# Moving three small tiles so that all large tiles of a hybrid decoder layer start at one remainder of 512 bytes

## The chip, the cores and the metric

The kernel runs on one core of a Trainium2 chip. The metric is the device time of one execution in microseconds; lower is better. A time shown is the median of several executions.

## The reference

One layer of a hybrid decoder on 512 tokens of width 1024, in float32. A normed input goes through one wide projection; a block-sparse attention branch and a gated linear recurrence branch follow; they are merged by sigmoid gates, projected, added to the input, and a gated embedding is added.

```python
xn = rmsnorm(h, norm_gain)
aq, ak, av, ag, bq, bf, bi, bg, gate_a, gate_b = split(xn @ w_in)    # 8 parts of 512 columns, 2 of 1024
ya = moba_attention(rmsnorm(aq) , rmsnorm(ak), av, rel_bias)          # 8 heads of 64
ya = (ya * silu(ag)) @ w_up_a
yb = hgrn2_chunkwise(silu(bq), (1 - lb) * sigmoid(-bf), bi, log_f)    # 4 heads of 128
yb = (rmsnorm(yb, hgrn_out_gain) * silu(bg)) @ w_up_b
h = h + (sigmoid(gate_a) * ya + sigmoid(gate_b) * yb) @ w_out
h = h + (p @ w_ple) * sigmoid(h @ w_ple_gate)
```

## The kernel before

Activations lie transposed: 128 features on the partitions, 512 tokens along the free axis, one tile of 2048 bytes a partition for each 128 features. Every large product is made of three TensorE matmuls in a reduced float32 format, high part by high part, high by low, low by high. So each operand exists as a high and a low tile: `wh`, `wl` for weights, `gh`, `gl` for the input times its gain, `xh`, `xl` for the normed input, `ybh`, `ybl` and `yah`, `yal` for the two branches, `mh`, `ml` for the merged value, `hh`, `hl` for the sum after the output projection, `ph`, `pl` and `pwh`, `pwl` for the embedding and its weights. ScalarE makes the high part by a copy, VectorE the low part by a subtraction (`split`, `scale_split`, `w_split`).

A projection of 128 output features is `mm3`, 8 blocks of 128 input features times 3 matmuls, 24 in all, each with 128 stationary columns and 512 moving ones. There are two orders. `proj_tr` (bf, bq, bg, ag, ga, gb), `up` (ub, ua) and the last two stages (h, g) hold a 128-column slice of the weights stationary and move the activations. `proj_tok` (bi, av, aq, ak) holds 128 tokens of the activations stationary and moves 512 weight columns. The last block of g is done in two halves of 256 columns.

Weights come by DMA from the SyncE queue into two `w` buffers, and are split two tiles ahead of their use into three buffers each for `wh` and `wl`. TensorE's order is written out by hand (`ORDER`, and generators that `tick` starts at due times); the other engines' order is set by a scheduler with priorities. Between the projections TensorE works on small matmuls of the attention (`s`, scores; `pt`, transposes of the softmax weights p; `o`, values) and of the recurrence (`lpb`, `lpa`, `hktp`, `hds`, `hop`).

`column_norms` sums a 128x512 tile over the partitions: a transpose of 32x32 blocks, a reduction to 128x16, three additions of 32-row groups, an inverse square root, and the way back. It is called five times, once for the input (`x_norm`) and once for each head of the recurrence (`hgrn_out`). Its three tiles of 128x16 (`sums`, `y`, `t_`; 64 bytes a partition) come from tag `n16` of the pool `sb`, with 3 buffers.

The pool `cst` lies ahead of the pool `sb` in SBUF; within a pool the tiles lie one after the other, in `sb` by tag in the order in which tags are first used, so each tag's place follows from the sizes of those ahead of it.

Of the kernel before, what the change touches and what calls it, by code (L numbers as in the profile page):

```python
# [11 lines left out]
F32 = mybir.dt.float32  # L12
# [45 lines left out]
def hybrid_layer_kernel(  # L58
# [18 lines left out]
    cst = ctx.enter_context(tc.tile_pool(name="cst", bufs=1))  # L77
# [4 lines left out]


    BUFS = {"w": 2, "wh": 3, "wl": 3, "A": 16, "R": 4, "X": 16, "YB": 8, "H": 10, "T": 3, "Q": 4, "QM": 2, "QX": 2, "KT": 2, "P": 4, "PT": 2,
            "PT0": 2, "PT2": 2, "SG": 4, "YS": 1, "VV": 8, "s32": 1, "st": 1, "ps": 8, "n16": 3}

    def unit(tag, name, dt=F32, shape=(128, 512)):
        return sb.tile(list(shape), dt, tag=tag, bufs=BUFS[tag], name=name)

    def bank(tag, name):  # L90
        return psum.tile([128, 512], F32, tag=tag, bufs={"mm": 4, "g": 2, "a": 2}[tag], name=name)
# [169 lines left out]
    def rsqrt(y, t, ms):  # L261

        A.activation(t, ms, AF.Ln, bias=epsc[0:t.shape[0], 0:1])
        A.activation(y, t, AF.Exp, scale=-0.5)
        V.scalar_tensor_tensor(t, ms, EPS, y, op0=OP.add, op1=OP.mult)
        V.tensor_tensor(t, t, y, op=OP.mult)
        V.tensor_scalar(t, t, -0.5, 1.5, op0=OP.mult, op1=OP.add)
        V.tensor_tensor(y, y, t, op=OP.mult)
# [15 lines left out]

    gh, gl, xh, xl = [], [], [], []
    rt = cst.tile([128, NT], F32, name="rt")

    def x_gain(k0, k1):
        for k in range(k0, k1):
            h_ = unit("A", f"gh{k}", R)  # L290
            l_ = unit("A", f"gl{k}", R)
            scale_split(h_, l_, xr[k], gain[:, k:k + 1])
            gh.append(h_)
            gl.append(l_)
# [26 lines left out]
    def column_norms(src, n, name, tag):  # L321


        u = unit(tag, name + "u")
        sums = unit("n16", name + "s", shape=(128, 16))
        y = unit("n16", name + "y", shape=(128, 16))
        t_ = unit("n16", name + "t", shape=(128, 16))
        g = [slice(32 * i, 32 * i + 32) for i in range(4)]
        V.transpose(u, src)
        V.tensor_reduce(sums, u.rearrange("p (b j) -> p b j", j=32), axis=AX.X, op=OP.add)  # L330
        V.tensor_tensor(sums[g[0]], sums[g[0]], sums[g[1]], op=OP.add)
        V.tensor_tensor(sums[g[2]], sums[g[2]], sums[g[3]], op=OP.add)
        V.tensor_tensor(sums[g[0]], sums[g[0]], sums[g[2]], op=OP.add)
        V.tensor_scalar(sums[g[0]], sums[g[0]], 1.0 / n, None, op0=OP.mult)
        rsqrt(y[g[0]], t_[g[0]], sums[g[0]])
        for i in range(1, 4):
            V.tensor_copy(y[g[i]], y[g[0]])
        z = unit(tag, name + "z")
        V.tensor_copy(u.rearrange("p (b j) -> p b j", j=32), y[:, :, None].to_broadcast([128, 16, 32]))
        V.transpose(z, u)  # L340
        return y, z

    def x_norm():
        with tc.high_priority(offset=AHEAD):
            y, rstd = column_norms(ssum, D, "xn", "YB")
            for g in range(4):
                V.tensor_copy(rt[32 * g:32 * g + 32], y[0:32].rearrange("p (t g) -> p t g", g=4)[:, :, g])
            x_normalise(rstd)
        yield RT
        for t in range(NT):  # L350
            A.activation(vb[t], vb[t], AF.Copy, scale=rt[:, t:t + 1])
# [22 lines left out]
    def proj_tr(i, name):  # L374
        ws = weight(w_tr[i])
        ps = bank("mm", name)
        mm3(ps, ws[0], ws[1], xh, xl, KD)
        return ps
# [186 lines left out]
    def hgrn_out(h, vb):  # L565
# [33 lines left out]
        with tc.high_priority(offset=AHEAD):  # L599
            A.activation(t, op_, AF.Square)  # L600
            y = column_norms(t, 128, f"h{h}n", "Q")[1]
            V.scalar_tensor_tensor(o, op_, ogain[:, h:h + 1], y, op0=OP.mult, op1=OP.mult)
# [253 lines left out]
    def up(i, n, ys, name):  # L856
        ws = weight(w_up[n, i])
        ps = bank("mm", name)
        mm3(ps, ws[0], ws[1], [y[0] for y in ys], [y[1] for y in ys], 4)
        return ps  # L860
# [3 lines left out]
    for kind, i in ORDER:  # L864
# [6 lines left out]
        elif kind == "ub":  # L871
            drain(f"yb{GH - 1}")
            ps = up(1, i, yb, f"ub{i}")
            V.tensor_tensor(sg["gb", i], ps, sg["gb", i], op=OP.mult)
        else:
            ps = proj_tr({"ga": 16, "gb": 24}[kind] + i, f"{kind}{i}")
# [3 lines left out]
    for n in range(KD):  # L880
        ga, gb = sg["ga", n], sg["gb", n]
        drain(f"ya{HPAIRS - 1}")
        ps = up(0, n, ya, f"ua{n}")
# [9 lines left out]
    for n in range(KD):  # L893
# [3 lines left out]
        ps = bank("mm", f"h{n}")  # L897
        mm3(ps, ws[0], ws[1], mh, ml, KD)
        t = unit("H", f"hf{n}")
# [8 lines left out]
    for k in range(2):  # L908
        t = unit("A", f"pf{k}")
# [6 lines left out]
    for n in range(KD):  # L916
# [10 lines left out]
        for i in range(parts):  # L927
# [8 lines left out]
            ps = bank("mm", f"g{n}_{i}")  # L936
# [3 lines left out]
            t = unit("Q", f"sg{n}_{i}")  # L940
# [71 lines left out]
```

## Time and profile before

| | |
|---|---|
| median of 3 runs | 472.62 us (472.6 to 473.32) |
| the profiled execution | 472.75 us, span 470.6 us |
| TensorE clock granted | 0.999 |
| TensorE matmul, weight load | 465.4 us (99%), 382.7 us (81%) |
| VectorE, ScalarE, GpSimd | 317.4 us (67%), 267.0 us (57%), 13.1 us (3%) |
| HBM traffic | 102 GB/s over the span |

The profile is of one execution; its span is the time from its first instruction to its last, and some 2.2 us of the execution's time lie around it. PE is TensorE's matmuls, PEld its weight loads, DVE VectorE, ACT ScalarE. Matmuls are pipelined and their ends modelled, so that a stage's speed is read from start to start. The chain that ended last is followed back from the last instruction, at each step to what released it or to the instruction before it on its engine.

### The profile page before, as it was taken

How to read it: one execution, taken by the hardware profiler on the slowest of the kernel's cores; microseconds unless marked ns; L12 is line 12 of the kernel's file. 1: busy time of each engine (PE TensorE's matmuls, PEld its weight loads, DVE VectorE, ACT ScalarE, POOL GpSimd, SP SyncE). 2: the span in 40 equal slices, each digit the busy share in tenths (PEclk: the TensorE clock that was granted, in tenths of full speed). 3: DMA queues.
4: the chain of work that ended last, by engine and by line, in shares of the span. 5: the costliest groups of instructions: out<-in, count | busy, mean ns of one | idle time of the engine just before them, and what ended most of it. 6: DMA issues, size and time to landing. Idle time of an engine off the chain costs nothing.

```text
span 470.6 us, 7271 instructions
## 1 busy us (share of the span) xinstructions
PE 465.4 (99%) x2762; PEld 382.7 (81%) x2762; DVE 317.4 (67%) x669; ACT 267.0 (57%) x471; POOL 13.1 (3%) x34
## 2 busy tenths in 40 slices
PE   9999999999999999999999999999999999999996
PEld 7888888788888888788888888888888888888886
DVE  4899468869889888977898485244559844544232
ACT  5856656567688876958686677454345422333201
POOL 0013000000000010000000000000000000000000
PEclk9999999999999999999999999999999999999999
DMA  8542333213423333131332333122534644222211
GB/s 266 193 134 90 99 106 108 91 47 112 139 86 135 114 71 127 61 100 53 107 106 80 107 98 104 47 67 67 180 91 134 204 162 147 92 89 96 84 45 45
DMA packets 19026, 50.41 MB, mean 107 GB/s; under 512 B 2352, under 2 KB 2992, under 8 KB 18992
## 3 DMA queue, kind: packets, MB, share of 16 engines
q1 hardware_dynamic: 18848, 49.95, 32.8%
q8 instruction: 21, 0.34, 0.3%
q14 instruction: 13, 0.11, 0.1%
q10 hardware_dynamic: 144, 0.01, 0.0%
HBM read 45.75 MB, written 2.10 MB: 102 GB/s over the span
## 4 chain that ended last, share of the span: by engine, by line
PE 96%; DVE 1%; DMA 1%; SPq 0%; ACT 0%; issue 0%; DVEq 0%
PE ga L252 10%; PE g L252 9%; PE h L252 9%; PE gb L252 9%; PE ak L393 5%; PE bg L252 5%; PE bq L252 5%; PE bf L252 5%; PE aq L393 5%; PE ag L252 5%; PE ua L252 5%; PE ub L252 5%; PE av L393 5%; PE bi L393 4%; PE pe L252 2%; PE s L697 2%
## 5 line engine op out<-in xcount | busy, mean ns | idle before, releaser
L235 ACT ACTIVATE wh<-wf 128x1024 fp32r<-128x1024 f32 (+1 forms) x78 | 75.8, 971 | 109.5 <-PE h L252 18.6
L236 DVE TENSOR_TENSOR wl<-wf,wh 128x1024 fp32r<-128x1024 f32 (+1 forms) x78 | 87.3, 1120 | 49.4 <-ACT wh L235 48.9
L252 PE MATMUL g<-hl,wh 128*128 128x512 f32 (+1 forms) x72 | 26.5, 368 | 0.0
L252 PE MATMUL g<-hh,wl 128*128 128x512 f32 (+1 forms) x72 | 26.5, 368 | 0.0
L252 PE MATMUL g<-hh,wh 128*128 128x512 f32 (+1 forms) x72 | 26.5, 368 | 0.0
L252 PE MATMUL gb<-xh,wh 128*128 128x512 f32 x64 | 26.3, 411 | 0.0
L252 PE MATMUL ga<-xh,wh 128*128 128x512 f32 x64 | 25.9, 405 | 0.0
L252 PE MATMUL gb<-xl,wh 128*128 128x512 f32 x64 | 25.3, 395 | 0.0
L252 PE MATMUL ga<-xh,wl 128*128 128x512 f32 x64 | 25.3, 395 | 0.0
L252 PE MATMUL ga<-xl,wh 128*128 128x512 f32 x64 | 25.3, 395 | 0.0
L252 PE MATMUL gb<-xh,wl 128*128 128x512 f32 x64 | 25.2, 394 | 0.0
L252 PE MATMUL h<-mh,wh 128*128 128x512 f32 x64 | 24.9, 389 | 0.0
L252 PE MATMUL h<-mh,wl 128*128 128x512 f32 x64 | 24.9, 389 | 0.0
L252 PE MATMUL h<-ml,wh 128*128 128x512 f32 x64 | 24.9, 389 | 0.0
L704 DVE CUSTOM_DVE_ANT_0 p<-s,bias 128x128 f32<-128x128 f32 (+3 forms) x32 | 14.9, 485 | 13.5 <-PE s L697 13.5
L706 ACT ACTIVATE p<-p,ps 128x128 f32<-128x128 f32 (+3 forms) x32 | 17.7, 554 | 10.1 <-DVE ps L704 10.1
L719 ACT ACTIVATE ptS<-pt 128x384 f32<-128x384 f32 (+1 forms) x24 | 12.5, 522 | 12.4 <-PE pt L715 12.3
L900 DVE TENSOR_TENSOR hf<-h,xres 128x512 f32<-128x512 f32 x8 | 5.5, 691 | 18.2 <-PE h L252 18.2
L252 PEld LDWEIGHTS g<-hh,wh 128*128 128x128 f32 x72 | 13.5, 188 | 2.6
L252 PEld LDWEIGHTS g<-hh,wl 128*128 128x128 f32 x72 | 13.5, 188 | 2.6
L252 PEld LDWEIGHTS g<-hl,wh 128*128 128x128 f32 x72 | 13.5, 187 | 2.5
L942 DVE TENSOR_TENSOR sg<-sg,pe 128x512 f32<-128x512 f32 (+1 forms) x9 | 5.6, 625 | 14.4 <-ACT sg L941 12.3
(371 smaller groups left out, 1262.1 us busy)
## 6 DMA issues: line engine op xcount, KB each, us to landing
wf<-in_w_tr_dram SPq DMA_DIRECT2D x32, 512.0 KB, 3.3
wf<-in_w_tok_dram SPq DMA_DIRECT2D x15, 512.0 KB, 3.3
wf<-in_w_up_dram SPq DMA_DIRECT2D x16, 256.0 KB, 2.6
wf<-in_w_o_dram SPq DMA_DIRECT2D x8, 512.0 KB, 3.3
wf<-in_w_g_dram SPq DMA_DIRECT2D x8, 512.0 KB, 3.3
bias<-in_brow_dram SPq DMA_DIRECT2D x8, 256.0 KB, 3.4
xres<-in_xT_dram SPq DMA_DIRECT2D x8, 256.0 KB, 2.8
xr<-in_xT_dram SPq DMA_DIRECT2D x7, 256.0 KB, 4.4
```

The lines of the kernel that those rows point to most:

```text
L235: A.activation(hi, wraw[i], AF.Copy)
L236: pin(V.tensor_tensor(lo, wraw[i], hi.bitcast(F32), op=OP.subtract))
L252: PE.matmul(ps, a[:, k, :], b[k], start=(n == 0), stop=(n == tot - 1))
L393: PE.matmul(banks[t], a[:, s_], b[:, kk, :], start=(k == 0 and i == 0), stop=(k == KD - 1 and i == 2))
L697: PE.matmul(sp[:, o:o + nk], qn[h][:, qs], k_[:, :nk], start=(i == 0), stop=(i == 1))
L704: V.tensor_tensor_reduce(p_, sp[:, o:o + nk], T[:, nk - 1::-1], -1.0, 3e38, OP.add, OP.min, st[:, 0:1])
L706: A.activation(p_, p_, AF.Exp, bias=st[:, 0:1], scale=-1.0, accum_out=st[:, 1:2])
L719: A.activation(pt, tp[:, :n * 128], AF.Copy)
L900: V.tensor_tensor(t, ps, xres, op=OP.add)
L942: V.tensor_tensor(t[:, :w], t[:, :w], pe[:, s_], op=OP.mult)
```

## The change

The three small tiles are made once, in the pool `cst`, and all five calls of `column_norms` use them. The tag `n16` is gone from `sb`.

```diff
-            "PT0": 2, "PT2": 2, "SG": 4, "YS": 1, "VV": 8, "s32": 1, "st": 1, "ps": 8, "n16": 3}
+            "PT0": 2, "PT2": 2, "SG": 4, "YS": 1, "VV": 8, "s32": 1, "st": 1, "ps": 8}
...
     rt = cst.tile([128, NT], F32, name="rt")
+    n16 = [cst.tile([128, 16], F32, name=f"n16{c}") for c in "syt"]
...
         u = unit(tag, name + "u")
-        sums = unit("n16", name + "s", shape=(128, 16))
-        y = unit("n16", name + "y", shape=(128, 16))
-        t_ = unit("n16", name + "t", shape=(128, 16))
+        sums, y, t_ = n16
```

In the built programs every engine has the same instructions in the same order with the same waits, and differs in addresses alone. `cst` grows by 3 x 64 = 192 bytes a partition, and the tags of `sb` that lay ahead of `n16` move up by 192 (as do the six small tiles of `qk_norm` at the end of `cst`); from tag `X` on, at byte 124800, nothing moves. The remainders of the tiles' start addresses by 512:

| tags | tiles | before | after |
|---|---|---|---|
| H, w, YB, A, wh, wl, VV (bytes 5824 to 124607) | xr, hf, raw weights; ybh, ybl, mh; gh, gl, qs, kh, kl, yah, yal, ml, ph, pl; weights; values | 192 | 384 |
| X (124800 to 157567) | xh, xl, hh, hl | 384 | 384 |
| QM, s32, Q, QX, P, PT, KT, st, R, SG, T (157568 to 217983) | among them p, hq, hkt, st, pwh, pwl | 384 | 384 |
| PT0, PT2, YS (above 218239) | transposed p of two kinds, ya | 128 | 128 |
| `ident`, `sc` in `cst` | identity, scores of the recurrence | 288 | 288 |
| the three small tiles | sums, y, t_ | 192, 256, 320 | 448, 0, 64 |

For the matmuls of 512 columns this gives:

| matmuls | stationary, moving | before | after |
|---|---|---|---|
| bi, av (96 each) | gh or gl, weights | 192, 192 | 384, 384 |
| aq, ak (96 each) | xh or xl, weights | 384, 192 | 384, 384 |
| bf, bq, bg, ag (96 each), ga, gb (192 each) | weights, xh or xl | 192, 384 | 384, 384 |
| ub, ua (96 each) | weights, ybh or ybl; yah or yal | 192, 192 | 384, 384 |
| h (192) | weights, mh or ml | 192, 192 | 384, 384 |
| g (168, and 48 of 256 columns) | weights, hh or hl | 192, 384 | 384, 384 |
| pe (42, and 12 of 256 columns) | pwh or pwl, ph or pl | 384, 192 | 384, 384 |

## The prediction, made before the changed kernel ran

> **What bounds the kernel now.** I read the page first: the busy shares, the clock and the chain of waits by engine.
>
> ```profile
> span 470.6 us, 7271 instructions
> ...
> PE 465.4 (99%) x2762; PEld 382.7 (81%) x2762; DVE 317.4 (67%) x669; ACT 267.0 (57%) x471; POOL 13.1 (3%) x34
> ...
> PEclk9999999999999999999999999999999999999999
> ...
> PE 96%; DVE 1%; DMA 1%; SPq 0%; ACT 0%; issue 0%; DVEq 0%
> ```
>
> TensorE (PE) is busy for 99% of the span, its clock is granted in every slice, and the chain that ended last is PE for 96%. Next, the list of what PE waits for, which has three rows:
>
> ```profile
> PE warm L147 <- PEq L999: 0.8, 1, 0.8
> PE pt L715 <- DVE p L708: 0.3, 1, 0.3
> PE bi L393 <- ACT wh L189: 0.2, 1, 0.2
> ```
>
> So PE waits 1.3 us in all. The time is the sum of its steps, from the start of one matmul to the start of the next. The chain in order of time (start, length, what, number of instructions) gives their length stage by stage:
>
> ```profile
> 27.76 21.76 PE av L393 x96
> 49.52 5.60 PE bf L252 x24
> 60.72 22.40 PE aq L393 x96
> ...
> 110.03 1.38 PE ak L393 x6
> 111.41 5.60 PE bg L252 x24
> ...
> 345.16 22.27 PE ua L252 x96
> 367.44 43.52 PE h L252 x192
> 410.95 1.37 PE pe L252 x6
> 412.33 5.60 PE g L252 x24
> 417.93 1.40 PE pe L252 x6
> ...
> 460.60 5.46 PE g L252 x48
> ```
>
> Divide each length by its count. All rows but the last are matmuls of 512 columns in the same number format. av takes 21.76 / 96 = 226.7 ns and h 43.52 / 192 = 226.7 ns; bf, bg and g take 5.60 / 24 = 233.3 ns, aq 22.40 / 96 = 233.3 ns, pe 1.37 / 6 = 228 ns and 1.40 / 6 = 233 ns. The stages h and g are the same loop over the same weight buffers, av and aq the same function; neither pair differs in shape. What differs is where the operands lie. By the table in the section on the change, av and h have the stationary and the moving operand at one remainder of 512 bytes (192), while bf, bg, aq and g pair 192 with 384. It does not matter which of the two is the stationary one: aq has it at 384, bf at 192. ua, at 192 and 192, has 22.27 us for 96; that row also holds the start of its stage, and even so it is below 233.3 ns (232.0).
>
> Both operands are indeed read at once, as the instructions in order of time show: the next weight load (PEld) starts with the running matmul.
>
> ```profile
> 300.55 0.39 PE L252 MATMUL ga<-xl,wh 128*128 128x512 f32 x1
> 300.55 0.19 PEld L252 LDWEIGHTS ga<-xh,wl 128*128 128x128 f32 x1
> 300.78 0.40 PE L252 MATMUL ga<-xh,wl 128*128 128x512 f32 x1
> ```
>
> (ga steps 0.23 us; the 0.39 is a modelled end.) The eight slices of a weight tile start 512 bytes apart; h uses all of them and still averages 226.7 ns, so distances in whole multiples of 512 bytes cost nothing.
>
> **The change, part by part.** No instruction is removed, added or moved, and no wait: both programs hold the same instructions with the same semaphore waits on every engine. column_norms already took the same three slots in each of its five calls, so sharing them adds no wait. What is left is addresses.
>
> *Wide matmuls that come to one remainder.* bf and bq 192, bg and ag 192, ga and gb 384, aq and ak 192, g 168 (seven blocks of 24), pe 42: 1170 instructions. I take 233.3 - 226.7 = 6.67 ns each where the row shows 233.3. About 48 of ak run in short pieces like the row at 110.03 (1.38 / 6 = 230 ns) and save some 3.3 ns, and the 42 of pe save 5 ns as the middle of 228 and 233. Sum: 1080 x 6.67 = 7.20, 48 x 3.3 = 0.16, 42 x 5 = 0.21, together 7.6 us. All of it lies on PE, which is the path. The ends for this term are 0 (addresses do nothing) and 1170 x 6.67 = 7.8 us; a loss is a rival below. No row shows a wide matmul with both operands at 384. I take the price of the rows that share a remainder, since a relation between the operands is what the rows separate.
>
> *Wide matmuls that stay at one remainder* (bi, av, ua, ub, h: 576, from 192 to 384): nothing, at the same argument.
>
> *Narrow matmuls.* The last block of g has 256 columns and unequal remainders and takes 5.46 / 48 = 113.8 ns, half of 227.5; there is no penalty to remove. At 128 columns:
>
> ```profile
> 104.58 0.67 PE hds L579 x6
> ...
> 107.08 1.39 PE ak L393 x6
> ...
> 108.91 0.22 PE hop L594 x2
> ```
>
> hds (192 with 384) takes 112 ns an instruction, hop of line 594 (384 with 384) 110 ns. The 2 ns, over the 240 records of hds, hop and o, would be 0.5 us either way; I take 0, since the chain prints hundredths and 0.22 / 2 is uncertain by more than that.
>
> *VectorE (DVE) and ScalarE (ACT).* Their tiles shift too. Groups by line and shape, before, whose operands differ in remainder (hl: 192, 384 into 384), agree (ml: 192, 192) and agree at 384 (pwl):
>
> ```profile
> L190 DVE TENSOR_TENSOR hl<-hf,hh 128x512 fp32r<-128x512 f32 x8 | 5.5, 684 | 0.0
> L190 DVE TENSOR_TENSOR ml<-sga,mh 128x512 fp32r<-128x512 f32 x8 | 5.4, 684 | 0.0
> L190 DVE TENSOR_TENSOR pwl<-pw,pwh 128x512 fp32r<-128x512 f32 x4 | 2.8, 688 | 0.1
> L189 ACT ACTIVATE hh<-hf 128x512 fp32r<-128x512 f32 x8 | 4.9, 617 | 0.0
> L189 ACT ACTIVATE mh<-sga 128x512 fp32r<-128x512 f32 x8 | 4.9, 625 | 4.5 <-DVE sga L888 4.5
> ```
>
> 684, 684 and 688 ns, 617 and 625 ns: no effect, and both engines have cover. If 8 ns did fall on every DVE instruction, it would count where DVE is full, in the 41 and 42 instructions of the two stretches shown next: 0.7 us either way. I take 0.
>
> *What is late next.* A faster PE reaches its waits earlier. Weight splits come first: the shortest lead in a stage that speeds up is at ag.
>
> ```profile
> 233.54 1.22 DVE L236 TENSOR_TENSOR wl<-wf,wh 128x1024 fp32r<-128x1024 f32 x1
> ...
> 239.76 0.40 PE L252 MATMUL ag<-xh,wh 128*128 128x512 f32 x1
> ```
>
> That tile is done at 234.8, 5.0 us ahead, and each split starts when PE frees a buffer, so the lead moves along with PE. The tight place is the wait for the softmax weights p. Two stretches by stage (start:end, then length, PE, PEld, DVE, ACT busy), and the rows at their ends:
>
> ```profile
> 183.00:199.50 16.50, 16.30 (x105) 13.26 (x103) 16.40 (x41) 14.27 (x28) 0.43 (x2) 1.00 0.20 67
> 234.00:250.80 16.80, 16.77 (x107) 13.63 (x105) 16.80 (x42) 14.20 (x28) 0.20 (x1) 1.00 0.29 94
> ...
> 199.56 0.61 PE L715 MATMUL pt<-ident,p 128*128 128x128 f32 x3 [0.25 <-DVE p L708]
> ...
> 250.43 0.54 DVE L708 TENSOR_SCALAR p<-p,ps 128x128 f32<-128x128 f32 x2
> ...
> 250.85 0.61 PE L715 MATMUL pt<-ident,p 128*128 128x128 f32 x3
> ```
>
> DVE is busy for 16.40 of 16.50 us and 16.80 of 16.80 us ahead of these two transposes, so p can't come earlier than DVE's work allows. PE gains (16.5 - 4) / 0.233 = some 54 x 6.67 ns = 0.36 us in each stretch and waits it off again; with the lags of two engines I take 0.4 each, 0.8 us. The list of PE's waits names no other transpose of p.
>
> Sum: 7.6 - 0.8 = 6.8 us. The profiled execution took 472.75 us (span 470.6), 0.13 above the median of 472.62. 472.75 - 6.8 = 465.95, rounded to 466.0.
>
> **The rivals.**
>
> *No effect.* The trace separates "X, PT and T tiles" from "the others" as well as it separates remainders: all the slow groups have one operand in the upper part of the memory (X starts at 124800) and the other below. If the distance or the place costs the 6.67 ns, the change moves nothing that matters and the time is 472.6. Against it: bf, aq and g each read all 16 X tiles, which are spread over 32 KB, and come to the same 233.3 ns. The Trainium skill speaks for this outcome in "TensorE: Matmul & The Clock Gate", Part 2, step 1: TensorE has two independent read ports, so that loading the next weights takes no bandwidth from the running matmul. By that rule how the two operands lie to each other could not matter, and after would equal before, 472.6. The trace does not fit it well: 226.7 against 233.3 ns in otherwise equal loops needs some coupling to where operands lie. Chance 0.10.
>
> *Slower: 384 itself is the costly place.* Perhaps a wide matmul costs 233.3 ns as soon as either operand is at 384. Then the 1170 keep their price and the 576 of bi, av, ua, ub and h rise by 6.67 ns: 576 x 6.67 = 3.8 us, 476.6. Every row fits this; against it only that a stationary read of 512 bytes and a moving read of 2048 would have to cost the same. It decides from 231.1 ns for a pair at 384 and 384, where 1170 x (231.1 - 233.3) and 576 x (231.1 - 226.7) cancel. Chance 0.07.
>
> *The gain is swallowed.* If DVE sets the pace of all of 110 to 251 us instead of two stretches, the 494 wide matmuls there give nothing: 7.6 - 494 x 6.67 ns = 4.3 us, 468.4. Against it is PE's list of waits, with one wait for p in it. Chance 0.05.
>
> That the change does not reach its tiles is excluded for all wide pairs by the addresses; PT0, PT2, YS and the identity stay at 128 and 288, but feed only matmuls of 128 columns or none.
>
> **How the numbers follow.** The forecast has 0.78. Its own bounds are 472.75 - 7.8 = 465.0 with no new wait, 0.5 below that if the narrow matmuls gain, and a gain of 7.6 - 2.4 = 5.2 us, 467.6, if the waits cost three times what I take. Stretched from 464.5 to 468.0 it also holds some of the swallowed case; no effect and slower, 0.17 together, are left out. Two tenths of a per cent, 0.9 us, is about what this measurement can tell from no change. Faster: 0.78 + 0.05 = 0.83; same 0.10; slower 0.07.
>
> **What would show it.** Right: bf, bg and g at 5.44 us for 24 in the chain, aq at 21.76 for 96, h and av unchanged at 43.52 and 21.76, and a wait of PE for p of 0.6 to 0.8 us at each of the two transposes. h and av at 233 ns would show the slower rival, bf still at 5.60 with av at 21.76 the one without effect. bf at 5.44 with a longer list of PE waits would show the swallowed gain.

## The result and the profile after

The changed kernel takes 468.26 us in the median of 4 runs (467.6 to 469.1) against 472.61 us (472.58 to 473.32, 4 runs) for the kernel before: a ratio of 0.9903, with a 95% interval of 0.9891 to 0.9916. It is faster by 4.35 us. 6.6 were forecast, and 468.26 lies just outside the range of 464.5 to 468.0.

The page of the profiled execution (467.6 us, the shortest of the four) has these lines for the span, the engines and the chain that ended last:

```profile
span 465.4 us, 7271 instructions
...
PE 459.4 (99%) x2762; PEld 382.6 (82%) x2762; DVE 317.2 (68%) x669; ACT 266.8 (57%) x471; POOL 13.1 (3%) x34
...
PE 96%; DVE 3%; DMA 1%; issue 0%; SPq 0%; DVEq 0%
```

PE still sets the time. The chain in order of time, after (start, length, what, count):

```profile
27.16 21.76 PE av L392 x96
48.92 5.44 PE bf L252 x24
...
59.80 21.92 PE aq L392 x96
...
109.72 5.44 PE bg L252 x24
...
363.18 43.54 PE h L252 x192
406.71 1.36 PE pe L252 x6
408.07 5.44 PE g L252 x24
...
455.03 5.76 PE g L252 x48
```

The wide stages that had 5.60 us for 24 matmuls (bf, bg, g) now have 5.44, aq 21.92 for 22.40, pe 1.36 for 1.37 to 1.40; av and h, whose operands lay together before as well, stay at 21.76 and 43.5. That is the step of 226.7 ns that was forecast. For aq 21.76 was forecast: its 19th step is 335 ns long in after, which no step of aq was before, and the next nine are 225 to 236. The last row went the other way: the 48 matmuls of 256 columns took 5.46 us before,

```profile
460.60 5.46 PE g L252 x48
```

and take 5.76 now, 120.0 for 113.6 ns each. The list of what PE waits for:

```profile
PE pt L714 <- DVE p L707: 1.2, 2, 0.6
PE warm L147 <- PEq L998: 0.8, 1, 0.8
```

The waits for p grew from 0.3 us in one place to 1.2 in two. What came out less than forecast are the stages that small matmuls interrupt. The chain in ga, before (three rows) and after (three rows):

```profile
278.85 2.80 PE ga L252 x12
...
282.11 4.20 PE ga L252 x18
...
286.63 2.80 PE ga L252 x12
```

```profile
275.36 2.76 PE ga L252 x12
...
278.57 4.08 PE ga L252 x18
...
282.98 2.76 PE ga L252 x12
```

Before, all pieces run at 233.3 ns a matmul. After, this piece of 18, which follows two score matmuls of 512 columns, runs at 226.7, and the pieces of 12, which follow transposes, at 230.

All of this from start to start, matmul by matmul, in the two profiled executions (us; minus is faster):

| part | forecast | measured |
|---|---|---|
| 1170 wide matmuls that come to one remainder | -7.57 | -5.76 |
| of these g, pe (never interrupted) | -1.33 | -1.33 |
| of these ga and gb | -2.56 | -1.60 |
| of these bf, bq, bg, ag, aq, ak | -3.68 | -2.83 |
| PE's waits for p | +0.8 | +0.85 |
| matmuls of 256 columns (g 0.31, pe 0.04) | 0 | +0.35 |
| all other matmuls from av on | 0 | -0.06 |
| sum from av on | -6.8 | -4.63 |

The first stage, bi, was 0.53 us shorter as well, but not by the change: in the traces of after and of seven variants below whose matmuls are the same up to there, av starts at any time from 27.16 (after) to 28.39 us. So from av on the traces say 4.6, the medians 4.35.

### The profile page after: what moved, and what is told of

Same layout as the page of the kernel before. It is cut to its first block, busy times and chain, and to the rows that moved or that the text cites. A ratio compares the mean times of both kernels' runs of the same rounds, so it can differ in the third digit from the quotient of the medians.

```text
span 465.4 us, 7271 instructions
## 1 busy us (share of the span) xinstructions
PE 459.4 (99%) x2762; PEld 382.6 (82%) x2762; DVE 317.2 (68%) x669; ACT 266.8 (57%) x471; POOL 13.1 (3%) x34
## 4 chain that ended last, share of the span: by engine, by line
PE 96%; DVE 3%; DMA 1%; issue 0%; SPq 0%; DVEq 0%
PE g L252 9%; PE h L252 9%; PE gb L252 9%; PE ga L252 9%; PE ua L252 5%; PE ak L392 5%; PE bq L252 5%; PE aq L392 5%; PE ub L252 5%; PE bf L252 5%; PE bi L392 5%; PE bg L252 5%; PE av L392 5%; PE ag L252 5%; PE pe L252 2%; PE s L696 2%
```

## The experiments

**Is it the place or the relation?** The first variant moves all large tiles of after together from 384 to 0, by 128 bytes of padding in the constants.

```diff
     n16 = [cst.tile([128, 16], F32, name=f"n16{c}") for c in "syt"]
+    cst.tile([128, 32], F32, name="pad")
```

> The changed kernel with 128 more bytes of padding at the end of the pool of constants: all large tiles up to T start at remainder 0 of 512 instead of 384, nothing else differs. Theory 'relation' (only the distance between the stationary and the moving operand, taken by 512, counts): the chain shows bf and g at 5.44 us for 24, av at 21.76 and h at 43.5, and the time is that of the changed kernel, 468.3 within 0.8 us. Theory 'place' (the remainder itself counts, and 384 happens to be a good one): the steps differ from 226.7 ns, by up to 6.7 ns each way on 1746 matmuls, so up to 11.6 us away.

Measured: 467.77 us (467.66 to 468.34, 4 runs), ratio 0.9897 (0.9880 to 0.9913). Every group of wide matmuls has the step that it has in after within 0.5 ns from av on, and so have the 256-column ones (120.0 ns), and PE waits 1.2 us for p. So 384 is not special.

The second keeps the sharing and pulls the tiles apart again; the third keeps the small tiles in their tag, as before, and pushes the large tiles together.

```diff
@@ after, for shared_but_apart
+    cst.tile([128, 80], F32, name="pad")
...
+            unit("padx", "padx", shape=(128, 48))    # ahead of the X tiles
@@ before, for unshared_but_together
+            unit("padx", "padx", shape=(128, 80))    # ahead of the X tiles
```

> After, with 320 bytes of padding in the constants and 192 ahead of the X tiles: the three small tiles are shared, but the large tiles lie at 0 and 192 bytes of remainder, 192 apart as before. If the distance is all, 472.6 us with bf, bg, g at 5.60 and av at 21.76. If sharing the small tiles (the column norms' own order and waits) has a part in the gain, between 468.3 and 472.

> Before, with 320 bytes of padding ahead of the X tiles and the small tiles left in their own tag: all large tiles at 192. If the distance is all, 468.0 us (467.6 to 468.6), with bf, bg, g at 5.44. If the sharing has a part, or 192 is worse than 384, between 469 and 472.

Measured: shared_but_apart 472.84 us, ratio 1.0002 (0.9992 to 1.0012); unshared_but_together 468.17 us, ratio 0.9902 (0.9887 to 0.9917). The chains of the two, in this order:

```profile
27.68 21.76 PE av L394 x96
49.44 5.60 PE bf L252 x24
...
460.52 5.46 PE g L252 x48
```

```profile
28.05 21.76 PE av L394 x96
49.81 5.44 PE bf L252 x24
```

The sharing of the three tiles is worth nothing, and the distance is worth all of it.

**Which distances cost?** Three variants of after put padding ahead of the weights (P bytes) and ahead of the X tiles (Q bytes), so that many pairs of operands lie apart by P, Q, or sums of them. One run each, for the steps in its trace.

```diff
+        if i == 0:
+            unit("padw", "padw", shape=(128, P // 4))   # ahead of the weights
...
+            unit("padx", "padx", shape=(128, Q // 4))   # ahead of the X tiles
```

> The changed kernel with padding of 32 bytes ahead of the split weights and 64 bytes ahead of the X tiles: av, ua and half of h have operands 32 bytes apart by 512, bf, aq and g 64 bytes apart. Theory 'any distance' (every unequal remainder costs the same): av and h at 233.3 ns a step (22.4 for 96, 44.8 for 192), bf and g at 233.3 (5.60 for 24). Theory 'lines' (operands must only share a line of 64 bytes or a bank of that size): the 32 byte pairs stay at 226.7, the 64 byte pairs go to 233.3. Theory 'far enough' (the penalty grows with the distance): both between 226.7 and 233.3, the second larger.

> The same with 96 bytes ahead of the split weights and 128 ahead of the X tiles: av, ua, h are 96 bytes apart, bf, aq, g 128 bytes. 'Any distance': 233.3 ns in all. 'Lines' of 128 bytes: 128 apart costs 6.7 ns and 96 may not. 'Far enough': larger than in the run with 32 and 64, below 233.3. The last block of g, 256 columns wide: 113 ns a step when the operands are apart, 120 when not, if what it showed at 192 and at 0 is a rule.

> The same with 160 bytes ahead of the split weights and 256 ahead of the X tiles: av, ua, h are 160 bytes apart, bf, aq, g 256 bytes. 'Any distance': 233.3 ns in all. If the remainder by 256 is what counts and not by 512, bf, aq and g stay at 226.7 ns (5.44 for 24).

Measured: 474.26, 475.71 and 472.29 us (before beside them 472.77). The mean step of the wide matmuls by how far the moving operand starts above the stationary one, modulo 256:

| distance | ns | groups |
|---|---|---|
| 0 | 226.7 | av, h, g of after; aq of apart_160_and_256 (256 apart) 227.0 |
| 32 | 233.3 | av |
| 64 | 229.3 to 231.6; 233.3 | g, bg, bf; aq of before |
| 96 | 233.3 | av; h in another variant |
| 128 | 232.2 to 233.3 | g, bf, aq |
| 160 | 234.3 | av, h |
| 192 | 233.3 | aq; g of before |
| 224 | 233.3 | h |

The row of 256 bytes is in the chain of apart_160_and_256, where av is 160 apart, aq 256, h 352:

```profile
28.37 22.49 PE av L395 x96
...
61.76 21.90 PE aq L395 x96
...
366.30 44.80 PE h L252 x192
...
411.10 1.40 PE pe L252 x6
412.50 5.47 PE g L252 x24
```

So 256 bytes apart is as good as 0 or 512, and what matters for the short step is whether the remainders by 256 are equal. They don't give the whole price of unequal ones: at 64, g (64 apart by 512) has 229.3 ns and aq of before (320 apart by 512, and with xh stationary) 233.3; which of the two differences counts, no run shows. The last two rows show more: g, 256 apart, has 5.47 us for 24 and not 5.44. The steps of this block, start to start, are 231, 231, 236, 228, 232, 231, and then 227, 227, 226 to its end. Ahead of it stands pe, whose operands lie 352 apart. The short step is something that a stream of matmuls runs into, and loses again.

**Why interrupted stages gained less.** Stage h is never interrupted in after. VectorE and ScalarE are not idle beside it, as the expectation has it: from 363 to 407 us of after they are busy for 56% and 34%. This variant puts three small matmuls behind each of its blocks but the last.

```diff
         mm3(ps, ws[0], ws[1], mh, ml, KD)
+        if n < KD - 1:
+            tp = bank("a", f"brk{n}")
+            for i in range(3):
+                PE.transpose(tp[:, i * 128:i * 128 + 128], ident, ident)
```

> After, with three more 128-column transposes of the identity behind each of the first seven of the eight blocks of stage h; their output is not used. The question is why the wide matmuls of ga and gb, in pieces between small matmuls, gained less than those of bg or g. Theory 'run-in': after any small matmul the first wide step is some 90 ns longer and the next 9 or 10 run at 228 to 236 ns, and only then at 226.7. Then the blocks 2 to 8 of h cost 5.44 + 0.09 + 9 x 0.005 = 5.57 us each, and with 7 x 3 x 0.11 for the transposes themselves h takes 43.5 + 2.3 + 0.9 = 46.7 us. Rival 'neighbours': ga and gb are slow since DVE and ACT work beside them; in h both are nearly idle, so only the first step of a block is longer, the second is at 227 at once, and h takes 43.5 + 2.3 + 0.6 = 46.4 us. The two are told apart by the 2nd to 10th steps of a block: 228 to 236 ns, or 226.7.

Measured: 471.28 us in one run. The chain, and the beginning of the second block in order of time (start, length, engine, line, what):

```profile
364.42 5.45 PE h L252 x24
369.87 0.33 PE brk L901 x3
370.19 5.49 PE h L252 x24
375.68 0.33 PE brk L901 x3
376.01 5.48 PE h L252 x24
```

```profile
370.26 0.40 PE L252 MATMUL h<-ml,wh 128*128 128x512 f32 x1
370.50 0.40 PE L252 MATMUL h<-mh,wl 128*128 128x512 f32 x1
370.73 0.39 PE L252 MATMUL h<-mh,wh 128*128 128x512 f32 x1
370.96 0.39 PE L252 MATMUL h<-ml,wh 128*128 128x512 f32 x1
371.19 0.40 PE L252 MATMUL h<-mh,wl 128*128 128x512 f32 x1
371.43 0.39 PE L252 MATMUL h<-mh,wh 128*128 128x512 f32 x1
```

The first wide step is 316 ns, the next are 233, 236, 224, 231, 236, 228, 233, 230, then 227, 227, 226 for the rest. In the other blocks it is 230, 231, 236, 228, 233, 231 and then 227. That is the run-in of theory 'run-in', 6 to 8 steps long and not 9 or 10, in a stage where the neighbours are the same as before the break; the rival, 226.7 from the second step on, is out. Both sums of the expectation were too high (h and its breaks take 410.52 - 364.42 = 46.10 us): I had counted the long first step as a loss of 90 ns, but the third transpose ahead of it shows 28 ns instead of 108, and the two together, 344 ns, are only 9 above 108 + 227. An interruption costs (46.10 - 7 x 0.33 - 43.54) / 7 = 0.04 us beyond its own matmuls.

**The waits for p, and fewer interruptions.** Two tests of the other terms, which also look for a better kernel. `LAG` sets how many steps behind the scores the transposes of p stand in PE's order; "merged" sets the next scores right behind the transposes.

```diff
-LAG = 2
+LAG = 3
@@ merged
-                yield AP * 0.4
...
-            yield AP * (0.6 if n >= LAG else 0.8)
+            yield AP * (1.0 if n >= LAG else 0.8)
```

> After, with the transposes of the softmax weights p one step later in PE's order (LAG 3 for 2). PE's two waits for p, 1.2 us in sum after the change, should fall below 0.3 us if p was merely late by half a microsecond, and the time to 467.2 us. If DVE is full throughout these stretches, the wait turns up at another place (the later one for p, for values, or for a weight split) and the time stays at 468.3 or goes above it.

> Before, with LAG 3 for 2, and the large tiles 192 bytes apart as before. The trace of before has 0.3 us of waiting of PE for p, against 1.2 us after. If LAG 3 only takes away waits for p, it is worth at most 0.3 us here: 472.3 to 472.7. If the order of LAG 3 saves something else (it gained 1.7 us on after), the same 1.7 us come here: 471.0.

> lag_3, with each head's next scores s right behind the transposes pt instead of 2.4 us later, so that some 20 interruptions of the wide matmuls fall away. In h_with_breaks an interruption cost (46.10 - 43.52) / 7 - 3 x 0.108 = 0.045 us beyond its own matmuls. If that is the price in the attention too, 20 x 0.045 = 0.9 us are saved: 465.6. Rival: the second interruption is free or the two banks of scores and transposes, now needed within 0.5 us, make PE wait: 466.5 or more, with waits of s in the list.

> After, with LAG 2 and the scores right behind the transposes. The scores start 2.4 us earlier against the transposes two steps on, so p has 2.4 us more: the waits for p (1.2 us) should go, and the saving of 0.9 us come beside it: 468.3 - 1.2 - 0.9 = 466.2. If DVE's load and not the place of s sets when p is ready, the waits stay at 1.2 us and the time is 467.4 or more.

| kernel | median us | ratio to before | PE's wait for p, us | interruptions of wide matmuls | av's start to the end, us |
|---|---|---|---|---|---|
| before | 472.8 | | 0.3 | 63 | 442.84 |
| before_lag_3 | 471.74 | 0.9978 (0.9968 to 0.9987) | none | 64 | 442.28 |
| after | 468.26 | 0.9903 (0.9891 to 0.9916) | 1.2 | 63 | 438.19 |
| lag_3 | 466.56 | 0.9866 (0.9851 to 0.9880) | none | 64 | 436.72 |
| lag_3_merged | 465.87 | 0.9851 (0.9837 to 0.9866) | none | 45 | 435.98 |
| lag_2_merged | 466.19 | 0.9857 (0.9841 to 0.9872) | none | 43 | 436.39 |

The last column is the span less the start of av in the same trace, so that the changing start is out of it; both are taken from the trace to the hundredth. The list of PE's waits in lag_3 has one row left:

```profile
PE warm L147 <- PEq L998: 0.8, 1, 0.8
```

LAG 3 is worth 1.47 us on after from av on (1.70 by the medians), of which 1.2 are the waits: p was only late by half a microsecond, and the wait did not turn up elsewhere. On before it is worth 0.56 us from av on, of which 0.3 are the wait; the medians say 1.06, between the 0.3 and the 1.7 of the two theories. The other 0.5 lies ahead of av in the trace (27.18 for 27.76), where traces of one and the same stage differ by more, and what it is stays open. The chain in ga after merging, where transposes and scores now stand in one gap:

```profile
276.70 0.33 PE pt L714 x3
277.03 0.35 PE s L696 x2
277.39 6.12 PE ga L252 x27
283.51 0.44 PE pt L714 x4
283.95 0.47 PE s L696 x2
284.42 6.15 PE ga L252 x27
```

27 in 6.12 us are 226.7 ns each. The second piece, 6.15 us, has a run-in behind its scores of 512 columns (235, 225, 230, 236, 229, 232, 231 and then 227), the first has none behind scores of 384; what decides this stays open. Against lag_3 there are 19 interruptions fewer, and the time from av on is 0.75 us shorter, 0.04 us for each, the price that the breaks in h gave; 0.9 had been expected. The intervals of the two ratios overlap, so the trace alone shows this. lag_2_merged lost its waits as expected, and of the expected 2.1 us 1.80 came from av on and 2.07 by the medians.

**A last version.** It puts the weights of the last block of g 192 bytes further, to take back the 256-column matmuls. For the room, each `wh` and `wl` buffer grows by 256 bytes, so half of them lie at 384 and half at 128 by 512: a second test of the 256.

```diff
-            hi = unit("wh", f"wh{i}", R, (128, kn, cols))
-            lo = unit("wl", f"wl{i}", R, (128, kn, cols))
+            pad = 48 if i == len(wseq) - 1 else 0
+            hi, lo = [unit(t, f"{t}{i}", R, (128, kn * cols + (64 if pad else 0)))[:, pad:pad + kn * cols]
+                      .rearrange("p (k c) -> p k c", k=kn) for t in ("wh", "wl")]
```

> lag_3_merged, with 256 bytes more for each of the six wh and wl buffers (so that they lie at 384 and 128 by 512, all at 128 by 256) and the weights of the last block of g 192 bytes into theirs, so that the 48 matmuls of 256 columns have their operands 192 bytes apart. If 256 bytes is the length that counts, every wide group keeps its 226.7 ns although half of the wh and wl lie 256 bytes from X by 512; if 512 is, those come to 233 and the time to some 469. If the 256-column steps go from 120.0 back to the 113.6 of before, the block takes 5.45 for 5.76 us: 465.87 - 0.31 = 465.6 us.

Measured: 465.48 us (465.18 to 465.63, 5 runs), ratio 0.9843 (0.9829 to 0.9856), the shortest of all. Its chain at the end:

```profile
447.45 5.44 PE g L253 x24
...
453.61 5.44 PE g L253 x48
```

The wide steps of g are 226.7 ns with 0 (96 of them) and 226.6 ns with 256 (72) between the operands: the 256 holds. The 48 narrow matmuls take 5.44 us, 0.32 less. Which distance does it for them is open: here the moving operand lies 64 above the stationary one by 256 (in before 192), yet in apart_32_and_64 the same 64 gave 117.8 ns.

## Why the prediction was right and wrong

- *What bounds the kernel, and the direction*: right. PE's steps are the time, and the wide ones fell from 233.3 to 226.7 ns. The two experiments that exchange sharing and distance show that the relation of the operands' places is the cause.
- *"1080 x 6.67 = 7.20"* is the step that failed: it gave the full 6.67 ns to stages whose wide matmuls stand in pieces between small ones. The uninterrupted g gave 1.12 of 1.12 us; ga and gb gave 1.60 of 2.56. Behind the transposes 5 to 9 steps run at 224 to 236 ns before the short step sets in (behind scores mostly none to three), and the steps of before, at 233.3, had next to nothing to lose there. In the groups that came together, the steps after (those that hold no interruption) exceed 226.7 ns by 1.5 us in sum, most of the 1.8 that are missing. The trace of before showed this price in ub, whose operands lay together already; its chain there:

```profile
320.36 2.77 PE ub L252 x12
...
323.48 4.11 PE ub L252 x18
...
327.92 2.75 PE ub L252 x12
```

  230.8, 228.3 and 229.2 ns, not 226.7. These rows, and not those of av and h, were the price for ga and gb: with ub's 2.77 and 4.11 for ga's 2.80 and 4.20, 30 matmuls save 0.12 us, 4 ns each, and 384 x 4 ns = 1.54 us is close to the 1.60 that ga and gb gave. I read ua's 232.0 ns only as a bound.
- *The wait for p*: right, +0.85 us for 0.8, in the two places named. VectorE (fourth entry after the window) is as full after as before in the two stretches, at the same times of the span:

```profile
183.00:199.50 16.50, 15.87 (x104) 13.10 (x103) 16.50 (x44) 13.61 (x26) 0.20 (x1) 1.00 0.29 96
234.00:250.80 16.80, 16.25 (x105) 13.27 (x103) 16.76 (x43) 12.72 (x25) 0.00 (x0) 1.00 0.30 102
```

  But "p can't come earlier than DVE's work allows" was too strong: LAG 3 removed the wait with VectorE's work unchanged (317.1 us busy for 317.2). That p then has a step more is the likely cause; the scheduler's order on VectorE and ScalarE changed in that run as well, so the run does not show it alone.
- *The narrow matmuls at 0*: right for 128 columns (the row of six hds has 0.67 us in both), wrong for 256: +0.35 us, the other part of the shortfall. That 113.8 ns is half of 227.5 did not mean that nothing could get longer.
- *512 bytes*: the pairs that were compared lay 0 or 192 apart, so the trace could not tell 512 from 256. It is 256.
- *The rivals*: none came. "No effect" would have been 472.6; what was drawn there from the rule of the Trainium skill ("TensorE: Matmul & The Clock Gate", Part 2, step 1), that loading weights takes no bandwidth from the running matmul, does not agree with these traces: 226.7 against 233.3 ns with the places of the operands alone changed. Whether it is the loading of weights that takes the 6.7 ns, no run shows. "384 is the costly place" fell with all_at_0. The swallowed gain forecast 468.4, close to what came, but by a list of waits that is not there: PE's waits for p grew by 0.9 us only. That its number comes close is chance.

## What to carry to other kernels

When the chain is one long stream of matmuls of 512 columns, divide each stage's length by its count, and compare stages of the same shape; if two prices appear, look at how the stationary and the moving tile lie to each other modulo 256 bytes, and pad to bring them together, but time blocks of 256 columns by themselves, since here they lost by it. Take the price of a stage from one that is interrupted equally often: in this kernel an interruption cost 0.04 us beside its own work, and putting two of them into one gap saved as much as that. A matmul stream that gets faster meets its producers earlier, and a step more of distance in the order was a cheap cure here.

## What the runs showed of the hardware

- Wide matmuls (128 x 128 by 512, reduced float32) step at 226.7 ns if stationary and moving operand start at one remainder of 256 bytes, and at 232 to 234 ns at the other distances tried, but for 64 bytes, which gave 229 to 232 in three groups and 233.3 in a fourth.
- The short step has to be run into: after transposes, or after matmuls whose operands lie apart, 5 to 9 steps of 224 to 236 ns come first. Score matmuls of 512 columns whose operands lie together do not disturb it where they stand between wide matmuls: behind the two in ga at 278.1 us of after the steps are 227, 227, 226 at once, as behind all six pairs of this kind. Behind the two pairs that follow other small matmuls, three and eight longer steps come.
- With 256 columns it is the other way round: 120.0 ns together, 113 to 114 ns in two layouts that lie apart, 117.8 and 118.8 in two others (64 and 128 bytes apart). Why, no run shows.
